# A Strassen matmul with RMS norm: GpSimd's adds to VectorE, row scaling to ScalarE, a plain last product, held row loads

## The chip, the cores and the metric

The kernel runs on one core of one Trainium2 chip. The metric is the device time of one execution in microseconds (us); lower is better. Three unprofiled runs of the kernel before took 246.84, 244.57 and 247.59 us: median 246.84.

## The reference

A product of two 2048 x 2048 matrices of float32, followed by a division of each row by its root mean square and a multiplication of each column by gamma:

```python
x = np.matmul(a, b)
rms = np.sqrt(np.mean(x ** 2, axis=-1, keepdims=True) + eps)
return (gamma * x / rms).astype(np.float32)
```

## The kernel before, in words

**Tiling.** The 2048 rows of `a` are 16 row blocks of 128; the 2048 columns of the result are four chunks of 512 (`CH`), two per half (`HALF` = 1024). A matmul instruction multiplies a 128x128 tile of `a` (transposed, it is the stationary operand) by a 128x512 tile of `b` into one PSUM bank. Depth is 16 tiles (`KT`), or 8 pairs (`KP`). `b` is kept whole in SBUF as bf16, `raw[j][kp]`, j being the half of the columns. Seven PSUM banks rotate as accumulators (`new_bank`, L304), an eighth serves transposes.

**Head (row blocks 0 to 3).** While `a` and `b` stream in by GpSimd's DMA queue (`load_head`, `load_b`, `load_later`), TensorE transposes four row blocks and multiplies them plainly (`head_matmul`, L300): first the left half of the columns, then the right half of blocks 0 to 2 (L350 to L357), then the two right chunks of block 3 (`r3`, L385 to L398). Meanwhile VectorE forms sums of quarters of `b` (`b_sums`, L218; `b_sums_in_place`, L225, which overwrites the two off-diagonal quarters of `raw[j][kp]` with sums).

**Strassen groups (row blocks 4 to 15).** Groups g = 2 (`G0`) to 7 hold two row blocks each, ra = 2g and rb = 2g+1. Each is done in two column halves, j = 0 and j = 1. A half (`group_half`, L401) is one level of Strassen's method: seven products of 8 matmuls in place of eight, in the order 2, 5, 1, 4, 3, 7, 6 (`product`, L230). Products 4 and 3 go on accumulating in the banks of products 2 and 5 (`start=False`), so product 4 can't start until ScalarE has copied product 2 out of its bank into the tile `t` (L414), and product 3 not until VectorE has added product 5 to `t` (L417). The four result chunks x11, x12, x21, x22 (t is x22's tile) come from these lines:

- L414 ScalarE copies product 2 to t; L417 and L421 VectorE adds product 5 and subtracts t from product 1;
- L424 ScalarE copies product 4 to x21 and squares it; L426 **GpSimd** forms x11 = t + x21;
- L429 ScalarE copies product 3 to x12 and squares it; L431 **GpSimd** forms t = t + x12;
- L435 and L440 VectorE adds products 7 and 6 to x11 and x22; ScalarE squares both.

`square` (L255) also accumulates the sum of squares of a row into `msq`. `finish(mb)` (L296) turns the four sums of a row block into 1/rms (VectorE reduce L271, add of eps L273, ScalarE square root L278, VectorE reciprocal L281), multiplies two halves of 1024 columns by it and by gamma on VectorE (L291), and writes each out by SyncE's queue (L294).

**Row blocks of a group to come.** Rows arrive by `load_block` (L116, GpSimd's queue, two float32 buffers `a32`). `row_norm` (ScalarE, L184 and L187) takes the norm of each row, `row_scale` (VectorE, L192 to L201) turns it to a power of two and writes the scaled rows as fp16 to `a16`, and `transpose_dma` (L173, SyncE's queue) transposes them by DMA into `at(mb)`. VectorE then forms the five sums of quarters of `a` that products 1, 2, 5, 6, 7 take (`a_sums`, L207 to L213).

**Order.** The schedule is written by hand: every engine works through its instructions in program order, and `hooks_of(g, j)` (L443) names the extra work that stands after each product of a half: hook n is placed between products. For j = 0 of a group from 3 on: hook 0 row_scale and transpose of block 2g+2, hook 1 row_norm of 2g+3, hook 3 row_scale and transpose of 2g+3 and finish of 2g-2. For j = 1: hook 0 the two row loads, hook 2 finish of 2g-1, hook 3 a_sums 2, 5, 1 of the next group, hook 5 row_norm of 2g+4, hooks 6 and 7 a_sums 7 and 6.

**Last half.** `last_half` (L491 on) is group 7, j = 1: the same seven products, with gamma multiplied in early, adds and multiplications on GpSimd (L517, L518, L523, L533), and five writes at the end (L534 to L546).

Of the kernel before, what the change touches and what calls it, by code (L numbers as in the profile page):

```python
# [17 lines left out]
def kernel(  # L18
# [156 lines left out]

    norm = {}
    eps_of = {}
# [12 lines left out]
    def row_scale(mb):  # L190
# [5 lines left out]
        e = stat_pool.tile([P, 1], FP32, name="e")  # L196
        nc.vector.tensor_scalar(out=e, in0=s, scalar1=s, scalar2=float(eps),
                                op0=ALU.mult, op1=ALU.mult)
        eps_of[mb] = e
        a16[mb] = a16_slot(mb)  # L200
        nc.vector.tensor_scalar_mul(out=a16[mb], in0=a32.pop(mb), scalar1=s)  # L201
# [23 lines left out]
    def b_sums_in_place(j, kp, eng=nc.vector):  # L225

        flat = raw[j][kp].rearrange("p t n -> p (t n)").rearrange("p (q n) -> p q n", q=4)
        eng.tensor_tensor(out=flat[:, 1:3, :], in0=flat[:, 1:3, :], in1=flat[:, 0::3, :],
                          op=ALU.add)
# [15 lines left out]
    msq = {}  # L245
    n_sq = {}

    def square(mb, src):
        if mb not in msq:
            msq[mb] = stat_pool.tile([P, NCH], FP32, name="msq")  # L250
            n_sq[mb] = 0
# [16 lines left out]
    def partial_rms(mb):  # L268

        part = stat_pool.tile([P, 1], FP32, name="part")  # L270
        nc.vector.reduce_sum(out=part, in_=msq[mb][:, 0:NCH - 1], axis=mybir.AxisListType.X)  # L271
        e = eps_of.pop(mb, None)
        nc.vector.tensor_scalar_add(out=part, in0=part, scalar1=float(eps) if e is None else e)  # L273
        return part

    def inverse_rms(mb, part):
        rms = stat_pool.tile([P, 1], FP32, name="rms")
        nc.scalar.activation(out=rms, in_=msq.pop(mb)[:, NCH - 1:NCH], func=ACTF.Sqrt,  # L278
                             bias=part, scale=1.0)
# [7 lines left out]
    def finish(mb):  # L287
        r = inverse_rms(mb, partial_rms(mb))
# [59 lines left out]
    for kp in range(KP):  # L348
# [12 lines left out]
        if kp == 4:  # L361
            row_norm(HB)
            row_scale(HB)
# [3 lines left out]
        if kp == 6:  # L367
            row_norm(HB + 1)
            row_scale(HB + 1)
# [6 lines left out]
    for r in range(HB - 1):  # L376
        for c, copy in ((2, nc.scalar.copy), (3, nc.vector.tensor_copy)):
            copy(out=x_chunk(r, c), in_=banks[r, c])

# [3 lines left out]

    squares2(0)
    r3 = HB - 1  # L385
    bank = new_bank()
    for kt in range(KT):
        head_matmul(bank, r3, 2, kt)
    finish(0)
    a_sums(G0, (2, 5, 1))  # L390
    squares2(1)
    nc.scalar.copy(out=x_chunk(r3, 2), in_=bank)
    bank = new_bank()
    for kt in range(KT):
        head_matmul(bank, r3, 3, kt)
# [192 lines left out]
```

## Time and profile before

| | us |
|---|---|
| median of three runs | 246.84 |
| the profiled execution, whole | 246.81 |
| its span in the profile | 245.0 |
| PE (TensorE) busy in the span | 217.9 |
| DVE (VectorE) busy | 179.8 |
| ACT (ScalarE) busy | 109.7 |
| POOL (GpSimd) busy | 82.8 |

The profile names engines PE, DVE, ACT, POOL and SP (SyncE); SPq, ACTq and POOLq are their queues. A row of the timeline gives the start and the length of an instruction in us, the engine, the line, the operation, the tile written and the tiles read, and in brackets how long the engine had been idle before it and what ended that. A wait row gives the engine and tile that waited, what it waited for, the total, the count and the longest. A window row gives, for a stretch of the span, each engine's busy time, the granted TensorE clock (1.00 is full) and what the DMA engines moved. The times of consecutive instructions overlap somewhat: an engine starts the next one before the last has left its pipeline, so the step from start to start is shorter than the length shown.

### The profile page before, as it was taken

The page shows a single profiled execution, that of the slowest core. Times are in us where ns is not written, and L with a number is a line of the kernel's source. Part 1 is how long each engine was busy: PE and PEld are TensorE (multiplying, and loading weights), DVE is VectorE, ACT ScalarE, POOL GpSimd, SP SyncE. Part 2 cuts the span into 40 slices and gives each one's busy share as a digit, 9 for nine tenths or more (in the row PEclk, how much of TensorE's full clock was granted, in tenths as well). Part 3 has the DMA queues.
Part 4 walks back from the last instruction along what each step waited for, and adds up shares of the span by engine and source line. Part 5 has one row for each costly group of instructions (what it writes and reads, how often), then busy time and mean ns, then how long its engine had stood idle before and what let it go on. Part 6 is the DMA issues. An engine that isn't in the chain of part 4 may idle for free.

```text
span 245.0 us, 2997 instructions
## 1 busy us (share of the span) xinstructions
PE 217.9 (89%) x1033; PEld 99.1 (40%) x1033; DVE 179.8 (73%) x304; ACT 109.7 (45%) x256; POOL 82.8 (34%) x71
## 2 busy tenths in 40 slices
PE   6789999998994999894999999999999999999800
PEld 1345444444441344341444444444444444444300
DVE  1144459835789989999868995999599959597760
ACT  3100004685279323627536843784377434343440
POOL 8333332100039417050354144504350515050640
PEclk9999999999997699998999999999999999999985
DMA  6999999999643068834889098809881934044026
GB/s 192 200 206 204 209 206 209 298 292 262 268 183 150 0 131 244 358 126 171 155 298 400 15 184 294 372 16 200 283 361 24 184 137 171 1 173 174 1 100 243
DMA packets 36560, 47.13 MB, mean 192 GB/s; under 512 B 21952, under 2 KB 26560, under 8 KB 34880
## 3 DMA queue, kind: packets, MB, share of 16 engines
q0 software_dynamic: 9648, 23.33, 37.4%
q1 hardware_dynamic: 26320, 21.50, 28.5%
q10 hardware_dynamic: 576, 2.10, 2.5%
q8 instruction: 8, 0.13, 0.2%
q14 instruction: 8, 0.07, 0.1%
HBM read 34.60 MB, written 16.78 MB: 210 GB/s over the span
## 4 chain that ended last, share of the span: by engine, by line
PE 57%; DVE 21%; DMA 13%; issue 3%; ACT 2%; POOL 2%; DVEq 0%; ACTq 0%; POOLq 0%
PE acc L238 46%; PE acc L301 10%; DMA b_7_84<-in_b_dram 7%; DMA b_3_80<-in_b_dram 6%; DVE s_105 L213 2%; DVE s_103 L213 2%; DVE early L223 1%; DVE s_104 L213 1%; DVE x_99 L291 1%; POOL early L107 1%; PE tbank L166 1%; DVE at_even L170 1%; DVE head_at L201 1%; ACT rms L278 1%; DVE x_102 L522 1%
## 5 line engine op out<-in xcount | busy, mean ns | idle before, releaser
L301 PEld LDWEIGHTS <-head_at 128*128 128x128 bf16 x256 | 24.9, 99 | 30.6 <-issue 2.6
L278 ACT ACTIVATE rms<-msq,part 128x1 f32<-128x1 f32 x16 | 4.7, 294 | 32.7 <-DVE part L273 32.6
L238 PEld LDWEIGHTS <-head_at 128*128 128x128 f16 x96 | 9.7, 101 | 16.1 <-issue 5.7
L238 PEld LDWEIGHTS <-s_104 128*128 128x128 f16 x96 | 9.6, 101 | 16.0 <-DVE s_104 L213 3.9
L426 POOL TENSOR_TENSOR x_97<-x_101 128x512 f32<-128x512 f32 x3 | 5.7, 1908 | 30.3 <-ACT x_101 L424 30.3
L238 PE MATMUL acc<-t_left,head_at 128*128 128x512 bf16 x48 | 12.2, 412 | 3.5 <-ACT x_101 L414 3.5
L426 POOL TENSOR_TENSOR x_95<-x_99 128x512 f32<-128x512 f32 x3 | 6.3, 2098 | 26.6 <-ACT x_99 L424 26.6
L238 PEld LDWEIGHTS <-s_105 128*128 128x128 f16 x96 | 9.7, 101 | 12.4 <-issue 1.9
L337 ACT COPY x_95<-acc 128x512 f32<-128x512 f32 x2 | 1.1, 589 | 30.4 <-PE acc L301 30.4
L238 PEld LDWEIGHTS <-at_even 128*128 128x128 f16 x96 | 9.4, 98 | 12.5 <-issue 1.2
L157 DVE COPY head_at<-tbank 128x1024 bf16<-128x1024 bf16 x7 | 4.8, 692 | 12.9 <-PE tbank L152 12.9
L238 PEld LDWEIGHTS <-s_107 128*128 128x128 f16 x96 | 9.4, 98 | 11.3
L238 PEld LDWEIGHTS <-s_106 128*128 128x128 f16 x96 | 9.4, 98 | 11.3
L238 PEld LDWEIGHTS <-s_103 128*128 128x128 f16 x96 | 9.4, 98 | 11.3
L426 POOL TENSOR_TENSOR x_96<-x_100 128x512 f32<-128x512 f32 x3 | 4.8, 1588 | 21.3 <-ACT sq L255 21.3
L238 PE MATMUL acc<-early,at_even 128*128 128x512 bf16 x48 | 10.8, 379 | 1.0 <-ACT x_100 L414 1.0
L238 PE MATMUL acc<-early,s_103 128*128 128x512 bf16 x48 | 11.3, 380 | 0.0
L238 PE MATMUL acc<-t_left,s_103 128*128 128x512 bf16 x48 | 11.3, 380 | 0.0
L238 PE MATMUL acc<-t_left,at_even 128*128 128x512 bf16 x48 | 10.9, 379 | 0.0
L238 PE MATMUL acc<-early,head_at 128*128 128x512 bf16 x48 | 10.8, 380 | 0.0
L255 ACT ACTIVATE sq<-x_95 128x512 bf16<-128x512 f32 x8 | 5.0, 631 | 8.1 <-DVE x_95 L435 8.0
L255 ACT ACTIVATE sq<-x_97 128x512 bf16<-128x512 f32 x8 | 5.0, 628 | 7.5 <-DVE x_97 L435 7.4
(320 smaller groups left out, 594.5 us busy)
## 6 DMA issues: line engine op xcount, KB each, us to landing
out_dram<-x_95 SPq DMA_DIRECT2D x4, 512.0 KB, 3.0
out_dram<-x_99 SPq DMA_DIRECT2D x4, 512.0 KB, 3.8
out_dram<-x_96 SPq DMA_DIRECT2D x4, 512.0 KB, 2.7
out_dram<-x_100 SPq DMA_DIRECT2D x4, 512.0 KB, 4.0
out_dram<-x_97 SPq DMA_DIRECT2D x4, 512.0 KB, 3.2
early<-in_a_dram POOLq DMA_DIRECT2D x7, 256.0 KB, 15.8
out_dram<-x_101 SPq DMA_DIRECT2D x3, 512.0 KB, 3.5
out_dram<-x_98 SPq DMA_DIRECT2D x3, 512.0 KB, 2.7
```

What stands on the lines that cost most here:

```text
L107: nc.gpsimd.dma_start(out=ah(kp), in_=a[0:HB * P, kp * W2:(kp + 1) * W2].rearrange("(r p) k -> p r k", p=P))
L157: nc.vector.tensor_copy(out=head_at[:, 2 * kp:2 * kp + 2, :, :], in_=view)
L166: nc.tensor.matmul(view[:, n, :], a16[mb][:, kt * P:(kt + 1) * P], identity_h, is_transpose=True, start=(n == 0), stop=(n == 7),)
L170: nc.vector.tensor_copy(out=at(mb)[:, g * 8:(g + 1) * 8, :], in_=view)
L201: nc.vector.tensor_scalar_mul(out=a16[mb], in0=a32.pop(mb), scalar1=s)
L213: nc.vector.tensor_tensor(out=s_sum[s], in0=x, in1=y, op=op)
L223: nc.vector.tensor_tensor(out=sums[j][:, n, kp, :], in0=x, in1=y, op=op)
L238: nc.tensor.matmul(bank, lhsT[:, kp, :], rhs, start=(start and kp == 0), stop=(kp == KP - 1), skip_group_check=not start)
L255: nc.scalar.activation(out=sq[:, 0:CH], in_=src, func=ACTF.Square, scale=inv_sqrt_n, accum_out=msq[mb][:, c:c + 1])
L278: nc.scalar.activation(out=rms, in_=msq.pop(mb)[:, NCH - 1:NCH], func=ACTF.Sqrt, bias=part, scale=1.0)
L301: nc.tensor.matmul(bank, head_at[:, kt, r, :], head_rhs(c, kt), start=(kt == 0), stop=(kt == KT - 1))
L426: nc.gpsimd.tensor_tensor(out=x11, in0=t, in1=x21, op=ALU.add)
```

## The change

1. The two adds of a Strassen half that GpSimd did (L426, L431) are VectorE's; so are the four `b_sums_in_place` that it did.
2. `row_scale` is split into `row_factor` (VectorE, four small operations; the scaled eps goes straight into an extra column of `msq`) and `row_apply` (the scaling of 2048 columns), which is VectorE's for blocks 4 to 7 and ScalarE's from block 8 on. For groups from 3 on they stand at hooks 0, 1, 3 and 4 of j = 0.
3. `finish` sums five columns of `msq` (eps is one) and takes the root of that: one VectorE operation fewer, and the reduce now needs all four squares.
4. At the entrance to the groups, the copies of the last head banks, a_sums, finish(0), row_norm of blocks 6 and 7, and the squares stand in another order; TensorE's order is the same. In group 2, finishes and `b_sums` stand at other hooks.
5. `load_after`: before the loads of the two row blocks for the group after next, GpSimd copies one column of the tile x22 of j = 0, which holds the loads until VectorE has written that tile.
6. The last half is a plain product: four chunks of 16 matmuls. The two quarters of `b` that had been overwritten by sums are loaded again (`load_again`, at hook 3 of j = 1 of group 6) into the two row buffers. Row block 14 is finished by `finish`; block 15's chunks are kept one by one, the last one straight from its bank, and written in four pieces of 512 columns.

The diff, cut to its core:

```diff
+    msq = {}
+    n_sq = {}
+
+    def new_msq(mb):
+        msq[mb] = stat_pool.tile([P, NCH + 1], FP32, name="msq")
+        n_sq[mb] = 0
+
+    for mb in range(HB):
+        new_msq(mb)
+        nc.gpsimd.memset(msq[mb][:, NCH:], float(eps))
+
+
...
-    def row_scale(mb):
+    def row_factor(mb):
         s = stat_pool.tile([P, 1], FP32, name="s")
         nc.vector.tensor_scalar_max(out=s, in0=norm.pop(mb), scalar1=1e-18)
         nc.vector.reciprocal(out=s, in_=s)
         nc.vector.tensor_single_scalar(out=s.bitcast(I32), in_=s.bitcast(I32),
                                        scalar=0x7F800000, op=ALU.bitwise_and)
-        e = stat_pool.tile([P, 1], FP32, name="e")
-        nc.vector.tensor_scalar(out=e, in0=s, scalar1=s, scalar2=float(eps),
+        new_msq(mb)
+        nc.vector.tensor_scalar(out=msq[mb][:, NCH:], in0=s, scalar1=s, scalar2=float(eps),
                                 op0=ALU.mult, op1=ALU.mult)
-        eps_of[mb] = e
+        factor[mb] = s
+
+    def row_apply(mb):
         a16[mb] = a16_slot(mb)
-        nc.vector.tensor_scalar_mul(out=a16[mb], in0=a32.pop(mb), scalar1=s)
+        if mb < HB + 4:
+            nc.vector.tensor_scalar_mul(out=a16[mb], in0=a32.pop(mb), scalar1=factor.pop(mb))
+        else:
+            nc.scalar.activation(out=a16[mb], in_=a32.pop(mb), func=ACTF.Copy,
+                                 scale=factor.pop(mb))
...
+    def inverse_rms(mb, partial=None):
+
         rms = stat_pool.tile([P, 1], FP32, name="rms")
-        nc.scalar.activation(out=rms, in_=msq.pop(mb)[:, NCH - 1:NCH], func=ACTF.Sqrt,
-                             bias=part, scale=1.0)
+        m = msq.pop(mb)
+        if partial is None:
+            tot = stat_pool.tile([P, 1], FP32, name="tot")
+            nc.vector.reduce_sum(out=tot, in_=m, axis=mybir.AxisListType.X)
+            nc.scalar.activation(out=rms, in_=tot, func=ACTF.Sqrt)
+        else:
+            nc.scalar.activation(out=rms, in_=m[:, NCH - 1:NCH], func=ACTF.Sqrt,
+                                 bias=partial, scale=1.0)
...
-    for r in range(HB - 1):
-        for c, copy in ((2, nc.scalar.copy), (3, nc.vector.tensor_copy)):
-            copy(out=x_chunk(r, c), in_=banks[r, c])
-
     def squares2(r):
         for c in (2, 3):
             square(r, x_chunk(r, c))
 
+    x_right = [[x_chunk(r, c) for c in (2, 3)] for r in range(HB - 1)]
+    for c in range(2):
+        nc.scalar.copy(out=x_right[0][c], in_=banks[0, 2 + c])
     squares2(0)
+    a_sums(G0, (2, 5))
+    finish(0)
+    nc.scalar.copy(out=x_right[1][0], in_=banks[1, 2])
+    for r, c in ((1, 1), (2, 0), (2, 1)):
+        nc.vector.tensor_copy(out=x_right[r][c], in_=banks[r, 2 + c])
+    a_sums(G0, (1,))
+    row_norm(HB + 2)
+    squares2(1)
+
     r3 = HB - 1
-    bank = new_bank()
-    for kt in range(KT):
-        head_matmul(bank, r3, 2, kt)
-    finish(0)
-    a_sums(G0, (2, 5, 1))
-    squares2(1)
-    nc.scalar.copy(out=x_chunk(r3, 2), in_=bank)
-    bank = new_bank()
-    for kt in range(KT):
-        head_matmul(bank, r3, 3, kt)
-    row_norm(HB + 2)
+    for c in (2, 3):
+        bank = new_bank()
+        for kt in range(KT):
+            head_matmul(bank, r3, c, kt)
+        nc.scalar.copy(out=x_chunk(r3, c), in_=bank)
+        if c == 2:
+            row_norm(HB + 3)
     squares2(2)
-    nc.scalar.copy(out=x_chunk(r3, 3), in_=bank)
...
-        nc.gpsimd.tensor_tensor(out=x11, in0=t, in1=x21, op=ALU.add)
+        nc.vector.tensor_tensor(out=x11, in0=t, in1=x21, op=ALU.add)
...
-        nc.gpsimd.tensor_tensor(out=t, in0=t, in1=x12, op=ALU.add)
+        nc.vector.tensor_tensor(out=t, in0=t, in1=x12, op=ALU.add)
...
+    pace = consts.tile([P, 1], FP32, name="pace")
+
+    def load_after(g, mb):
+
+
+        nc.gpsimd.tensor_copy(out=pace, in_=x_chunk(2 * g + 1, 1)[:, 0:1])
+        load_block(mb)
...
-        def scale(mb):
-            row_scale(mb)
+        def apply(mb):
+            row_apply(mb)
             transpose_dma(mb)
 
         more = g + 1 < NG
         if j == 0:
-            if more:
-                hook(0, scale, nxt)
-                hook(0 if g == G0 else 1, row_norm, nxt + 1)
             if g == G0:
-                for kp in range(KP // 2):
-                    hook(0, b_sums_in_place, 1, kp, nc.gpsimd)
+                hook(0, row_factor, nxt)
+                hook(0, apply, nxt)
+                hook(0, row_factor, nxt + 1)
                 hook(1, squares2, r3)
-                hook(1, a_sums, g, (7, 6))
-            if more:
-                hook(3, scale, nxt + 1)
-            if g == G0:
+                hook(2, apply, nxt + 1)
+                hook(2, a_sums, g, (7, 6))
                 hook(3, b_sums_in_place, 0, KP - 1)
                 hook(3, finish, 1)
-                hook(4, b_sums, 1, KP - 1)
+                hook(4, finish, 2)
+                hook(6, b_sums, 1, KP - 1)
+            elif more:
+                hook(0, row_factor, nxt)
+                hook(1, apply, nxt)
+                hook(1, row_norm, nxt + 1)
+                hook(3, row_factor, nxt + 1)
+                hook(3, finish, 2 * g - 2)
+                hook(4, apply, nxt + 1)
             else:
                 hook(3, finish, 2 * g - 2)
-                if not more:
-                    hook(5, finish, 2 * g - 1)
+                hook(5, finish, 2 * g - 1)
         else:
             if g == G0:
-                for kp in range(KP // 2, KP):
-                    hook(1, b_sums_in_place, 1, kp)
-            if g == G0:
-                hook(2, finish, 2)
-                hook(5, finish, r3)
+                for kp in range(KP):
+                    hook(1 + kp // 4, b_sums_in_place, 1, kp)
             else:
                 hook(2, finish, 2 * g - 1)
             if more:
                 hook(3, a_sums, g + 1, (2, 5, 1))
                 hook(6, a_sums, g + 1, (7,))
                 hook(7, a_sums, g + 1, (6,))
+            if g == G0:
+                hook(4, finish, r3)
             if g + 2 < NG:
-                hook(0, load_block, nxt + 2)
+                hook(0, load_after, g, nxt + 2)
                 hook(0, load_block, nxt + 3)
                 hook(5, row_norm, nxt + 2)
+            elif more:
+                hook(3, load_again)
         return hooks
 
+
+
+    b_again = {}
+
+    def load_again():
+        nc.gpsimd.tensor_copy(out=pace, in_=x_chunk(MB - 3, 1)[:, 0:1])
+
+        for q, cols in ((2, (2 * CH, 3 * CH)), (1, (3 * CH, N))):
+            raw_q = a_pool.tile([P, K], FP32, name="a32").bitcast(BF16)
+            b_again[q] = raw_q.rearrange("p (k n) -> p k n", n=CH)
+            rows_q = b.rearrange("(k t p) n -> p t k n", t=2, p=P)[:, q // 2]
+            nc.gpsimd.dma_start(out=b_again[q], in_=rows_q[:, :, cols[0]:cols[1]])
+
     def last_half():
...
+        def chunk(mb, c):
+            bank = new_bank()
+            for kt in range(KT):
+                q = 2 * (kt % 2) + c % 2
+                rhs = b_again[q][:, kt // 2] if q in b_again else b_quarter(1, kt // 2, q // 2, q % 2)
+                nc.tensor.matmul(bank, at(mb)[:, kt], rhs, start=(kt == 0), stop=(kt == KT - 1))
+            return bank
+
+        def keep(mb, c, bank):
+            x = x_chunk(mb, c)
+            nc.scalar.copy(out=x, in_=bank)
+            square(mb, x)
+
+        keep(ra, 2, chunk(ra, 2))
+        keep(ra, 3, chunk(ra, 3))
+        x = x_tile(rb, 0)
+        nc.vector.tensor_tensor(out=x, in0=x, in1=gamma_sb[:, 0:HALF], op=ALU.mult)
+        keep(rb, 2, chunk(rb, 2))
+        nc.vector.tensor_tensor(out=x_chunk(rb, 2), in0=x_chunk(rb, 2), in1=gam[2], op=ALU.mult)
+        finish(ra)
+        part = stat_pool.tile([P, 1], FP32, name="part")
+        nc.vector.tensor_scalar(out=part, in0=msq[rb][:, 0:1], scalar1=msq[rb][:, 1:2],
+                                scalar2=msq[rb][:, 2:3], op0=ALU.add, op1=ALU.add)
+        nc.vector.tensor_tensor(out=part, in0=part, in1=msq[rb][:, NCH:], op=ALU.add)
+        bank = chunk(rb, 3)
+        square(rb, bank)
+        r = inverse_rms(rb, part)
+        y = [x_chunk(rb, c) for c in range(NCH)]
+        nc.scalar.activation(out=y[0], in_=y[0], func=ACTF.Copy, scale=r)
+        nc.scalar.dma_start(out=rows(rb, 0, CH), in_=y[0])
+        nc.vector.scalar_tensor_tensor(out=y[3], in0=bank, scalar=r, in1=gam[3],
                                       op0=ALU.mult, op1=ALU.mult)
+        nc.sync.dma_start(out=rows(rb, 3 * CH, N), in_=y[3])
+        for c, queue in ((1, nc.sync), (2, nc.scalar)):
+            nc.vector.tensor_scalar_mul(out=y[c], in0=y[c], scalar1=r)
+            queue.dma_start(out=rows(rb, c * CH, (c + 1) * CH), in_=y[c])
```

75 lines of the change are left out of this document (10 added, 65 removed).

## The prediction

> **What bounds the kernel now.** I read the stretches first, cut where TensorE's work changes:
>
> ```profile
> 0.00:36.90 36.90, 31.97 (x171) 15.48 (x172) 13.66 (x32) 2.52 (x3) 15.95 (x27) 1.00 1.10 203
> ...
> 74.30:119.55 45.25, 37.32 (x154) 15.80 (x153) 43.30 (x66) 21.62 (x53) 16.52 (x9) 0.89 0.51 164
> 119.55:219.69 100.14, 100.14 (x465) 45.33 (x464) 82.63 (x130) 56.08 (x134) 36.81 (x24) 1.00 0.61 193
> 219.69:231.95 12.26, 12.26 (x57) 5.38 (x55) 9.23 (x14) 4.53 (x11) 3.66 (x3) 1.00 0.26 105
> 231.95:245.00 13.05, 0.00 (x0) 0.00 (x0) 4.13 (x8) 3.18 (x7) 3.36 (x2) 0.69 0.43 161
> ```
>
> After span and matmuls the columns are PE, PEld, DVE, ACT, POOL, clock, DMA share, GB/s. From 119.55 to 231.95 TensorE never pauses, at full clock: whatever other engines do there is worth nothing. Two stretches can give: 74.30 to 119.55, and the 13.05 us after the last matmul. Before 74.3 TensorE's order stays and the change moves nothing that its loads or transposes wait for. TensorE's waits and its timeline say what the first loses:
>
> ```profile
> PE acc L238 <- ACT x_101 L414: 3.5, 1, 3.5
> PE acc L238 <- DVE s_104 L213: 3.4, 1, 3.4
> PE acc L238 <- ACT x_100 L414: 1.0, 1, 1.0
> ```
> ```profile
> 73.90 0.59 PE L301 MATMUL acc<-b_7_92,head_at 128*128 128x512 bf16 x2
> 77.92 0.61 PE L238 MATMUL acc<-b_0_77,s_104 128*128 128x512 bf16 x1 [3.43 <-DVE s_104 L213]
> ...
> 83.40 0.38 PE L238 MATMUL acc<-b_5_82,s_105 128*128 128x512 bf16 x1
> ...
> 98.99 3.61 PE L238 MATMUL acc<-early,at_even 128*128 128x512 bf16 x16 [0.96 <-ACT x_100 L414]
> ...
> 109.34 1.89 PE L238 MATMUL acc<-t_left,s_103 128*128 128x512 bf16 x8
> 114.77 4.94 PE L238 MATMUL acc<-t_left,head_at 128*128 128x512 bf16 x16 [3.54 <-ACT x_101 L414]
> 119.55 0.38 PE L238 MATMUL acc<-b_0_77,s_107 128*128 128x512 bf16 x1
> ```
>
> At full clock a matmul takes 12.08/56 = 0.2157 us (the last half's 56, counted 12.26 with the last one's drain of 0.17), a product of 8 takes 1.73, a half 12.08. After 3.4 and 3.5 us of idleness matmuls run at half rate for a while: 77.92 to 83.40 holds 13 in 5.48, not 2.80 (2.68 lost), 114.77 to 119.55 holds 16 in 4.78, not 3.45 (1.33 lost). After 0.96 there is no loss. From start to start each wait is 0.16 longer than its idle time (109.34 + 1.73 = 111.07, to 114.77 is 3.70; likewise 3.59 and 1.12). Together 3.59 + 2.68 + 1.12 + 3.70 + 1.33 = **12.4 us** could go.
>
> **Why they stand there.** The first wait is for a sum on VectorE that takes 2.61 where the same sum takes 0.68 elsewhere, while GpSimd adds beside it (the multiply at 145.13, 2.30 for 1.28, is another case):
>
> ```profile
> 71.34 2.91 POOL L228 TENSOR_TENSOR b_0_85<-b_0_85 128x1024 bf16<-128x1024 bf16 x1 [5.11 <-PE acc L301]
> ```
> ```profile
> 75.26 2.61 DVE L213 TENSOR_TENSOR s_104<-at_even 128x1024 f16<-128x1024 f16 x1
> ...
> 130.81 0.68 DVE L421 TENSOR_TENSOR x_102<-acc,x_102 128x512 f32<-128x512 f32 x1
> 131.41 0.68 DVE L213 TENSOR_TENSOR s_104<-at_even 128x1024 f16<-128x1024 f16 x1
> ...
> 137.45 0.14 DVE L192 TENSOR_SCALAR s<-norm 128x1 f32<-128x1 f32 x1
> ...
> 138.14 1.28 DVE L201 TENSOR_SCALAR head_at<-a_1074,s 128x2048 f16<-128x2048 f32 x1
> ...
> 142.97 0.15 DVE L271 TENSOR_REDUCE part<-msq 128x1 f32<-128x3 f32 x1
> ...
> 143.73 0.16 DVE L281 RECIPROCAL r<-rms 128x1 f32<-128x1 f32 x1 [0.36 <-ACT rms L278]
> 143.93 1.28 DVE L291 SCALAR_TENSOR_TENSOR x_97<-x_97,r,gamma_sb 128x1024 f32<-128x1024 f32 x1
> 145.13 2.30 DVE L291 SCALAR_TENSOR_TENSOR x_98<-x_98,r,gamma_sb 128x1024 f32<-128x1024 f32 x1
> ```
>
> The other two are copies of t (L414) late on ScalarE, behind squares that wait for VectorE.
>
> **Prices**, as steps from start to start. VectorE: a sum or add 0.60 (130.81 to 131.41), a finish multiply 1.20 (143.93 to 145.13), a scaling as long as that (1.28), 1.20, factor 0.70 (137.45 to 138.14). The two adds taken from GpSimd read SBUF twice and have no free row on VectorE: as the PSUM add, 0.60, to half a finish multiply, 0.60; both ends agree. A finish: reduce 0.22, root 0.33 (143.40 to 143.73), reciprocal 0.20, two multiplies: 3.15. ScalarE:
>
> ```profile
> 137.02 0.63 ACT L255 ACTIVATE sq<-x_102 128x512 bf16<-128x512 f32 x1 [0.54 <-DVE x_102 L440]
> ...
> 137.65 0.57 ACT L414 COPY x_99<-acc 128x512 f32<-128x512 f32 x1
> 138.11 1.06 ACT L184 ACTIVATE sq<-a_1076 128x1024 bf16<-128x1024 f32 x1
> ...
> 140.47 0.29 ACT L187 ACTIVATE norm<-n_1198 128x1 f32<-128x1 f32 x1
> ...
> 143.40 0.29 ACT L278 ACTIVATE rms<-msq,part 128x1 f32<-128x1 f32 x1 [2.63 <-DVE part L273]
> ```
> ```profile
> L540 ACT ACTIVATE x_101<-x_101,r 128x1024 f32<-128x1024 f32 x1 | 1.1, 1148 | 0.3 <-DVE r L281 0.3
> ```
>
> A copy takes 0.48, 0.62 until its reader starts; a square 0.63, or 0.75 ahead of another (half of the norm's 2.36, less 0.43 for the 512 columns more); a norm 2.57 with its root. Scaling 2048 columns on ScalarE has no row. Squares grow by 0.43 per 512 columns (0.63, 1.06); two such steps more on the 1148 ns row give 2.0, a step of 1.92. Bounds: 1.8 (the square's 1.06 and two steps, less 0.1 of overlap) and 2.5 (four squares of 512). I take 1.92, from the row that scales.
>
> **The order laid out by hand**, each engine in program order with those prices, a product's reader starting 0.25 after TensorE can go on (200.70 + 1.73 = 202.43 to 202.68):
>
> ```profile
> 200.70 3.62 PE L238 MATMUL acc<-early,at_even 128*128 128x512 bf16 x16
> ...
> 202.68 0.58 ACT L424 COPY x_100<-acc 128x512 f32<-128x512 f32 x1 [2.12 <-PE acc L238]
> ```
>
> GpSimd no longer adds, so a sum costs 0.60 and the first group's s_2 is ready at 69: TensorE goes from 74.3 straight on. What decides next is again the copy of t, due 0.1 before product 4:
>
> | half | what stands ahead | t copied | TensorE due | wait |
> |---|---|---|---|---|
> | group 2, left | ScalarE from 66.1: 5 copies 2.4, 6 squares 4.5, norms 6 and 7 5.1, root 0.2, 1.3 of waiting for finish 0's reduce: 79.6 | 80.2 | 79.5 | 0.7 |
> | group 2, right | VectorE from 80.2: finish 1 and 2 6.3, 9 adds and sums 5.4, `b_sums(1, 7)` 1.1, a scaling 1.2: 94.2; then a square and the copy | 95.7 | 93.3 | 1.0 + 2.5 |
> | group 3, left | VectorE from 94.2: 8 in-place sums 4.8, 10 adds and sums 6.0, finish 3 3.15: 108.15; then a square and the copy | 109.7 | 107.8 | 1.9 |
> | group 3, right | ScalarE from 109.5: scaling, norm, VectorE's factor and reduce, root, copy, square, scaling, copy: 119.2; two adds 1.4, two squares 1.5, the copy | 122.65 | 121.8 | 0.9 |
> | group 4, left | VectorE from 122.65: finish 5, 10 adds and sums: 131.8; then a square and the copy | 133.3 | 134.7 | 0 |
> | group 4, right | as in group 3 | 146.3 | 146.8 | 0 |
>
> The 1.0 is product 1 of group 2, right: its last two matmuls need `b_sums(1, 7)`, now behind finish 2. New waits 0.7 + 1.0 + 2.5 + 1.9 + 0.9 = 7.0, so 12.4 - 7.0 = **5.5 us** won (unrounded), and the last half starts at 214.2, not 219.69. From group 4 a round from t to t takes 12.97 us for a left half and 10.68 for a right one, 23.65 against TensorE's 24.16: hidden with 0.5 us of cover. VectorE's two adds (1.2 a half), ScalarE's scalings (3.8 a group) and the finishes ride in that round and cost nothing while it is the shorter; beyond it each us costs one per group.
>
> **What else costs nothing.** The eps column's four memsets on GpSimd come while its queue waits for loads. On SyncE's queue the second transpose of a group moves behind the two writes of finish(2g-2); their last multiply ends at 141.6 in group 4, before the scaled rows (142.2).
>
> **Held loads.** The small copy on GpSimd waits for x22 of the left half, 144.6 in group 4, 15.1 after the group's start. Only the two load issues queue behind it on GpSimd. Rows of before (the last line is over all writes of the result):
>
> ```profile
> a_1293<-in_a_dram POOLq DMA_DIRECT2D x1, 1024.0 KB, 6.5
> a_1295<-in_a_dram POOLq DMA_DIRECT2D x1, 1024.0 KB, 8.5
> out_dram<-x_101 ACTq DMA_DIRECT2D x1, 512.0 KB, 3.8
> out_dram<-x_98 ACTq DMA_DIRECT2D x1, 512.0 KB, 5.6
> head_at<-head_at SPq DMA_TRANSPOSE x6, 4.4
> ```
> ```profile
> DMA to landing us min/median/max: 2.6/3.1/6.5
> ```
>
> They land at 151.2 and 153.2; the norm wants the first at 151.9. The second transpose, 142.2 + 4.4 = 146.6, is 4 us ahead of the sums at 150.7. Nothing on the path, though the loads start 2 us before that transpose is through. The reloaded quarters (2.1 MB written) are asked for about 192 and wanted at 214.4 and 217.6: with 2.1 MB of output among them, 4.2 MB at the 203 GB/s of the first 36.9 us, in which loads were never short of requests, take 20.7 us: to 213. They just fit.
>
> **The end.** GpSimd's adds and multiplies there go (L517 to L533), and eight matmuls come: 8 x 0.2157 = **+1.7**. TensorE ends at 228.1. Then, in the chain as before, square and root: block 15's third chunk is copied by 225.3, its gamma multiply (0.6), finish(14) (3.15) and the partial sum (0.4) hold VectorE to 229.4, later than the last square (228.9); root to 229.8, reciprocal 230.0, three multiplies of 0.6, 0.4 and 0.4 (512 columns; a third of a scaling's 1.20) to 231.5; the last write of 256 KB goes out at 231.6. Now:
>
> ```profile
> 237.54 0.36 ACTq L546 DMA_DIRECT2D out_dram<-x_98  x1
> ```
>
> It landed 5.6 later, at 243.1, and the span ran on 1.9 to 245.0. With half as much written behind the last matmul I take 3.8 (the x_101 row, 512 KB with others queued; bounds 2.6, the shortest write, and 5.6): 235.4, plus 1.9 is 237.2. The tail is 9.1, not 13.05: **-3.95**.
>
> Sum: 245.0 - 5.5 + 1.7 - 3.95 = 237.2; with 1.8 around the span (246.81 - 245.0) **239.0 us**. The profiled 246.81 and the median 246.84 are the same, so this is 3.2% under the median.
>
> **A rule weighed.** The 2.5 us wait lies between the rows with loss (3.4) and without (0.96). The Trainium skill, "TensorE: Matmul & The Clock Gate", Part 1, says that the clock falls to half after about one idle window of 3.4 us; the two rows agree. By that rule the wait costs no clock and the sum stays 239.0; by the row of 77.92 it would be 241.7.
>
> **Rivals.**
> A. *ScalarE and VectorE become the bound.* The round has 0.5 us of cover. With a scaling of 2.5 it is 24.8: 0.65 too long in groups 4 to 6, and 1.15 more in group 3; TensorE ends 3.1 later: **242.1 us**. For: the cover is thin, and 0.02 us more on each step of the two engines use it up as well. Against: the 1148 ns row. 20%.
> B. *A cold clock at the entrance.* The 2.5 us wait follows a 1.0 wait closely; if it halves the clock as after 3.43, 2.7 us are lost: **241.7 us**. 12%.
> C. *Slower: held loads come too late.* The norm would block ScalarE, with squares and the next t behind it. First load lands 6.5 after issue; the norm has 0.7, t then 1.9, of cover. From 2.6 us late on, each us costs one in each of four groups. At 13 us: (6.5 - 2.6) x 4 = 15.6, **254.6 us**; slower by 2% needs 12 us. Against: the loads of the rows above took 6.5 and 8.5. 4%.
> D. *The reload is late.* At 165 GB/s the second quarter lands at 217.5 and from there on each us late is one lost; at 145 GB/s it is 221; TensorE waits 3 us: **242 us**. 6%.
>
> **How the numbers follow.** My forecast (5.5 and 4 us won, 1.7 paid) has 58%, and its own scatter is +-2. The range reaches down to a scaling of 1.8, shorter waits and a tail with 2.6 (236.5, with the runs' scatter of 1.5 down to 235.0), up to A with a little more: 244.0. A measurement tells about 2% of this kernel from no change, 241.9 downwards. Faster: 0.53 of the forecast's 0.58, half of B and D, 0.09, and 0.12 of A's milder forms: 0.74. Slower: C and a hundredth for worse forms of A: 0.05. Same: 0.21.
>
> **What would show it.** Right: no GpSimd add; VectorE sums at 0.68 throughout; the wait for s_104 gone; waits for L414's copy of 0.5 to 2.5 us in groups 2 and 3 and none from group 4 on; the last half starting near 214, 64 matmuls, a tail near 9. Wrong: TensorE waiting once per group after 130 (A), matmuls 0.43 apart near 96 (B), norms waiting for loads (C), a wait for the reloaded quarters (D), or a tail that is still 12 us.

## The result and the profile after

The changed kernel takes 236.98 us (median of four runs, 236.82 to 237.10) against 246.54 us (four runs, 244.57 to 247.59): a ratio of 0.962, 95% interval 0.956 to 0.968. It is faster, by 3.8%; 239.0 us had been predicted. Times here are medians over the executions of a kernel; where some took over 1.5% longer than the quickest, as in run 5, the time and the ratio are those of the quicker ones.

The stretches of the changed kernel, cut at the same events as those of before (columns as there):

```profile
36.90:74.06 37.16, 35.83 (x188) 17.08 (x189) 26.76 (x59) 21.97 (x51) 3.57 (x6) 1.00 0.95 266
74.06:112.00 37.94, 35.06 (x151) 15.36 (x153) 32.43 (x61) 22.20 (x51) 3.38 (x3) 0.96 0.53 177
112.00:212.40 100.40, 99.59 (x454) 45.29 (x463) 74.10 (x137) 69.18 (x144) 5.69 (x12) 1.00 0.83 219
212.40:226.40 14.00, 13.93 (x64) 6.17 (x63) 5.66 (x9) 5.58 (x14) 0.00 (x0) 1.00 0.19 77
226.40:235.30 8.90, 0.00 (x0) 0.00 (x0) 3.69 (x8) 1.70 (x4) 0.00 (x0) 0.63 0.61 236
```

The last half starts at 212.40, 7.3 us before 219.69. It is 14.00 long for 12.26, and the tail 8.90 for 13.05. So -7.3 + 1.7 - 4.15 = -9.7, the whole difference of the two spans (235.3 and 245.0). DMA share in the third stretch rises from 0.61 (in 119.55 to 219.69) to 0.83, the bytes only from 193 to 219 GB/s. The reload is new there; why the DMA engines are busy so much longer no run shows.

TensorE's timeline, where it waits:

```profile
77.51 1.89 PE L256 MATMUL acc<-t_left,s_103 128*128 128x512 bf16 x8
79.47 3.61 PE L256 MATMUL acc<-t_left,at_even 128*128 128x512 bf16 x16
...
89.83 1.67 PE L256 MATMUL acc<-early,s_103 128*128 128x512 bf16 x7
91.97 0.38 PE L256 MATMUL acc<-early,s_103 128*128 128x512 bf16 x1 [0.46 <-DVE early L241]
94.53 5.30 PE L256 MATMUL acc<-early,at_even 128*128 128x512 bf16 x16 [2.18 <-ACT x_100 L431]
99.66 0.38 PE L256 MATMUL acc<-b_0_85,s_107 128*128 128x512 bf16 x1
...
120.89 3.40 PE L256 MATMUL acc<-early,head_at 128*128 128x512 bf16 x14 [0.28 <-ACT x_102 L431]
```

The wait of 3.4 us for s_104 is gone, and so is the one of 3.5 us for the copy of x_101. What is left are four of the five waits that the prediction laid out, smaller; after 121 TensorE waits for nothing. Behind the 2.18 us of idleness 16 matmuls take 99.66 - 94.53 = 5.13, not 3.45: 1.68 lost, at a granted clock of 0.67 in that stretch.

Rows of ScalarE, VectorE and GpSimd: the scaling (L218), an add that was GpSimd's (L448), and the held loads (L466 is the small copy, L116 a load).

```profile
108.21 2.00 ACT L218 ACTIVATE head_at<-a_848,s 128x2048 f16<-128x2048 f32 x1
110.12 1.04 ACT L196 ACTIVATE sq<-a_850 128x1024 bf16<-128x1024 f32 x1
```
```profile
90.29 0.68 DVE L448 TENSOR_TENSOR x_99<-x_99,x_95 128x512 f32<-128x512 f32 x1
90.90 0.68 DVE L452 TENSOR_TENSOR x_95<-acc,x_95 128x512 f32<-128x512 f32 x1
```
```profile
93.25 2.38 POOL L466 COPY pace<-x_99 128x1 f32<-128x1 f32 x1 [27.28 <-DVE x_99 L457]
95.57 0.53 POOL L116 DMA_DIRECT2D a_848<-in_a_dram  x1
...
119.53 0.18 POOL L466 COPY pace<-x_101 128x1 f32<-128x1 f32 x1 [22.90 <-DVE x_101 L457]
120.06 0.53 POOL L116 DMA_DIRECT2D a_1072<-in_a_dram  x1 [0.34 <-issue]
```

From start to start the scaling takes 1.91 and an add 0.61. Next come some DMA issues (the last figure is the time from issue to landing in us), the landing times of the transposes (L173), and the end:

```profile
a_1763<-in_b_dram POOLq DMA_DIRECT2D x1, 1024.0 KB, 12.5
a_1765<-in_b_dram POOLq DMA_DIRECT2D x1, 1024.0 KB, 19.5
out_dram<-x_102 ACTq DMA_DIRECT2D x1, 256.0 KB, 3.7
```
```profile
DMA to landing us min/median/max: 4.2/4.7/7.0
```
```profile
226.47 0.60 ACT L268 ACTIVATE sq<-acc 128x512 bf16<-128x512 f32 x1 [1.14 <-PE acc L547]
...
228.52 0.29 ACT L290 ACTIVATE rms<-msq,part 128x1 f32<-128x1 f32 x1 [1.35 <-DVE part L565]
...
230.62 0.35 ACTq L577 DMA_DIRECT2D out_dram<-x_102  x1
```

### The profile page after: what moved, and what is told of

Same layout as the page of the kernel before. It is cut to its first block, busy times and chain, and to the rows that moved or that the text cites. A ratio compares the mean times of both kernels' runs of the same rounds, so it can differ in the third digit from the quotient of the medians.

```text
span 235.3 us, 2970 instructions
## 1 busy us (share of the span) xinstructions
PE 215.1 (91%) x1021; PEld 99.0 (42%) x1041; DVE 156.6 (67%) x303; ACT 123.2 (52%) x264; POOL 28.7 (12%) x52
## 5 line engine op out<-in xcount | busy, mean ns | idle before, releaser
L256 PE MATMUL acc<-early,at_even 128*128 128x512 bf16 x47 | 12.5, 422 | 2.2 <-ACT x_100 L431 2.2
L288 ACT ACTIVATE rms<-tot 128x1 f32<-128x1 f32 x15 | 3.0, 203 | 21.5 <-DVE tot L287 21.5
L256 PEld LDWEIGHTS <-s_107 128*128 128x128 f16 x88 | 8.6, 98 | 10.4
L256 PEld LDWEIGHTS <-s_106 128*128 128x128 f16 x88 | 8.6, 98 | 10.4
L256 PEld LDWEIGHTS <-s_103 128*128 128x128 f16 x88 | 8.6, 98 | 10.4
L256 PEld LDWEIGHTS <-s_104 128*128 128x128 f16 x88 | 8.6, 98 | 10.4
L256 PEld LDWEIGHTS <-s_105 128*128 128x128 f16 x88 | 8.6, 98 | 10.4
L256 PEld LDWEIGHTS <-head_at 128*128 128x128 f16 x80 | 7.8, 98 | 10.0 <-issue 0.8
L256 PE MATMUL acc<-t_left,head_at 128*128 128x512 bf16 x48 | 10.8, 379 | 0.0
L256 PE MATMUL acc<-early,s_103 128*128 128x512 bf16 x40 | 9.6, 379 | 0.5 <-DVE early L241 0.5
L547 PEld LDWEIGHTS <-head_at 128*128 128x128 f16 x64 | 6.3, 98 | 7.5
L466 POOL COPY pace<-x_99 128x1 f32<-128x1 f32 x2 | 2.6, 1284 | 49.3 <-DVE x_99 L457 49.3
L204 DVE TENSOR_SCALAR s<-norm 128x1 f32<-128x1 f32 x12 | 1.8, 150 | 9.0 <-ACT norm L199 9.0
L256 PE MATMUL acc<-early,head_at 128*128 128x512 bf16 x31 | 7.2, 379 | 0.3 <-ACT x_102 L431 0.3
```

The source lines that it names most:

```text
L204: nc.vector.tensor_scalar_max(out=s, in0=norm.pop(mb), scalar1=1e-18)
L256: nc.tensor.matmul(bank, lhsT[:, kp, :], rhs, start=(start and kp == 0), stop=(kp == KP - 1), skip_group_check=not start)
L288: nc.scalar.activation(out=rms, in_=tot, func=ACTF.Sqrt)
L466: nc.gpsimd.tensor_copy(out=pace, in_=x_chunk(2 * g + 1, 1)[:, 0:1])
L547: nc.tensor.matmul(bank, at(mb)[:, kt], rhs, start=(kt == 0), stop=(kt == KT - 1))
```

## The experiments

Theory at the start: the gain at the entrance comes from GpSimd's adds and sums going and from the new order, the end brings some 2 us, and the held loads cost and bring nothing. Rivals: the hold is what pays, or the scaling on ScalarE. "After" is the changed kernel, "before" the other one; ratios are to runs of before on the same chip. "The hold" is the small GpSimd copy ahead of the row loads, "the entrance" the stretch from the end of the head to group 3.

### 1. The two adds back on GpSimd

```diff
-        nc.vector.tensor_tensor(out=x11, in0=t, in1=x21, op=ALU.add)
+        nc.gpsimd.tensor_tensor(out=x11, in0=t, in1=x21, op=ALU.add)
...
-        nc.vector.tensor_tensor(out=t, in0=t, in1=x12, op=ALU.add)
+        nc.gpsimd.tensor_tensor(out=t, in0=t, in1=x12, op=ALU.add)
```

> The changed kernel, with only the two adds of each Strassen half back on GpSimd. My theory: the 9.6 us come from two places, 7.3 up to the start of the last half (VectorE no longer slowed by GpSimd, and its work at the entrance of groups 2 and 3 in another order) and 2.5 at the end (shorter tail, less the 8 matmuls). By it the adds on GpSimd stretch VectorE's sums and finish multiplies again (0.68 to 1.7, 1.28 to 2.3), VectorE is the engine that is never idle in group 2, so the waits there grow by 1.5 to 3 us, and the round of ScalarE and VectorE, which had 0.5 us of cover, overruns in groups 3 to 6: 239 to 243 us. Rival (the adds only moved, TensorE hides them as it did before): 237 +-0.5.

239.13 us (ratio 0.968, 0.965 to 0.972), 2.15 over after and at the lower end of what I expected. Beside a GpSimd add a pair of finish multiplies takes 3.49 us, where run 7 has 2.48. The wait for b_sums grows from 0.46 to 1.28, and groups 4 and 5 get waits of 0.58 and 0.17 for sums. The waits of before do not come back: with the hold in place the adds alone are worth some 2 us.

### 2. The old last half

`last_half` as before, without `load_again`; the rest is after's.

> The changed kernel with the last half of the kernel before (seven products, GpSimd's adds and multiplications, five writes) and no second load of b. My theory: TensorE ends 1.7 us earlier, the tail is 13.05 again instead of 8.9: 237.0 - 1.7 + 4.15 = 239.4 us. Rival (the end gives nothing, everything came from the entrance): 235.3 us or 237.

239.96 us (ratio 0.972, 0.969 to 0.976): the plain end is worth 3.0 us here, in keeping with 4.15 - 1.74 = 2.4 from the two traces.

### 3. No hold

```diff
-        nc.gpsimd.tensor_copy(out=pace, in_=x_chunk(2 * g + 1, 1)[:, 0:1])
         load_block(mb)
```

> The changed kernel without the small GpSimd copy ahead of the row loads, so that they start as soon as their buffers are free. My theory: neither loads nor transposes are on TensorE's path (4 us of cover for the second transpose, 1.2 for the load): 237.0 +-0.5, the trace showing loads some 8 us earlier and transposes longer than the 4.7 us of now. Rival (the hold is what the change needs): transposes slowed past their 4 us of cover, sums late, 0.5 to 2 us per group lost, 239 to 245.

255.75 us (ratio 1.037, 1.031 to 1.043): 18.8 us over after, and slower than before. My theory fell, and the rival's 239 to 245 was too low as well. Rows of SyncE's queue, of ScalarE, the landing times of the transposes, and rows of TensorE:

```profile
81.16 10.96 SPq L173 DMA_TRANSPOSE head_at<-head_at  x1
92.21 5.29 SPq L306 DMA_DIRECT2D out_dram<-x  x4
```
```profile
103.21 0.59 ACT L431 COPY x<-acc 128x512 f32<-128x512 f32 x1 [9.46 <-DMA out_dram<-x]
```
```profile
DMA to landing us min/median/max: 4.2/11.5/19.5
```
```profile
103.85 5.22 PE L256 MATMUL acc<-early,at_even 128*128 128x512 bf16 x16 [11.76 <-ACT x L431]
138.91 3.63 PE L256 MATMUL acc<-b,s 128*128 128x512 bf16 x16 [2.21 <-DVE s L231]
...
166.27 3.63 PE L256 MATMUL acc<-b,s 128*128 128x512 bf16 x16 [2.03 <-DVE s L231]
```

The loads now go out at 76.97 and 81.63 (after: 95.57 and 96.09), beside the transposes. A transpose takes 11.5 us to land (median) instead of 4.7, and its issue holds SyncE's queue for up to 10.96. Four output writes stand behind it. The copy of t needs the tile that one of them reads: it waits 9.46 for that write, and TensorE 11.76 for the copy. At groups 4 to 6 TensorE waits 1.7 to 2.2 us for sums of late transposes.

### 4. All scaling on VectorE

```diff
-        if mb < HB + 4:
+        if mb < MB:
```

> The changed kernel with all row scaling on VectorE. My theory: a round of the two engines is then 22.9 us instead of 23.65, both under TensorE's 24.16 a group: 237.0 +-0.5, the scaling's place is worth nothing. Rival (VectorE, which took over GpSimd's adds, can't carry the scaling as well): waits for the copy of t or for sums from group 4 on, 0.5 to 1.5 us per group, 239 to 243.

236.39 us (ratio 0.957, 0.954 to 0.959): where the rows from block 8 on are scaled makes no difference that counts; if any, VectorE is 0.6 better. That rival fell.

### 5. Before, with nothing but the adds and sums moved to VectorE

```diff
-        nc.gpsimd.tensor_tensor(out=x11, in0=t, in1=x21, op=ALU.add)
+        nc.vector.tensor_tensor(out=x11, in0=t, in1=x21, op=ALU.add)
...
-        nc.gpsimd.tensor_tensor(out=t, in0=t, in1=x12, op=ALU.add)
+        nc.vector.tensor_tensor(out=t, in0=t, in1=x12, op=ALU.add)
...
-                    hook(0, b_sums_in_place, 1, kp, nc.gpsimd)
+                    hook(0, b_sums_in_place, 1, kp)
```

> The kernel before with one part alone: the two adds of each half and the four in-place sums of b taken from GpSimd to VectorE, nothing else. My theory: the wait for s_104 (3.6 us with 2.7 of slow clock) goes, since a sum takes 0.68 again; but VectorE's list at the entrance gets 2.4 us of sums and 1.2 us of adds per half longer in its old order, so the waits for the copy of t stay: 240 to 243 us, some 4 to 6 us won. Rival (the order is what matters, contention nothing): 246 +-1.

267.8 us (266.82 and 268.75; all four executions 266.82 to 281.13, median 273.52; ratio 1.087, 1.079 to 1.095): 21 us slower than before, where 4 to 6 us of gain had been expected. The trace is of the longest execution (span 279.4), so its waits sum to more than that. The part that was expected did come: the three sums of a whose first had made TensorE wait take 1.89 us together, where each took 2.6 in before.

```profile
73.02 1.89 DVE L213 TENSOR_TENSOR s<-at_even 128x1024 f16<-128x1024 f16 x3
```

In before, GpSimd's in-place sums stood beside them (71.34 to 82.37); its first add of a group came only at 91.03. So it was the in-place sums that made this wait. What went wrong stands in GpSimd's queue, in before and then in this run:

```profile
91.03 2.10 POOL L426 TENSOR_TENSOR x_95<-x_99 128x512 f32<-128x512 f32 x1 [8.67 <-ACT x_99 L424]
93.21 2.13 POOL L431 TENSOR_TENSOR x_99<-x_99,x_95 128x512 f32<-128x512 f32 x1
95.29 0.57 POOL L116 DMA_DIRECT2D a_840<-in_a_dram  x1
```
```profile
77.35 0.53 POOL L116 DMA_DIRECT2D a<-in_a_dram  x1 [11.46 <-DVE head_at L201]
```

In before a load stood behind the half's two adds in GpSimd's order, and so went out only at 95.29, when the transposes were through. Without the adds it goes out at 77.35, as soon as its buffer is free. Landing times of the transposes and rows of TensorE in this run:

```profile
DMA to landing us min/median/max: 4.5/12.6/24.9
```
```profile
109.94 6.49 PE L238 MATMUL acc<-early,at_even 128*128 128x512 bf16 x16 [17.99 <-ACT x L414]
147.81 6.34 PE L238 MATMUL acc<-b,s 128*128 128x512 bf16 x16 [3.75 <-DVE s L213]
184.17 5.24 PE L238 MATMUL acc<-b,s 128*128 128x512 bf16 x16 [9.30 <-DVE s L213]
```

New theory: GpSimd's adds were an unseen brake on the loads, and the hold puts it back. Runs 7 and 8 test that.

### 6. Before, with the plain end alone

This is before with `last_half` and `load_again` of after; the reload comes without its small copy.

> The kernel before with one part alone: the plain last half with the second load of two quarters of b (not held). My theory: 8 more matmuls, +1.7, and a tail of 8.9 for 13.05: 246.5 - 2.4 = 244.1 us. Rival (the reload comes late beside GpSimd's adds, or the tail was short only because GpSimd had stopped): 246 to 249.

244.51 us (10 executions; ratio 0.992, 0.989 to 0.994): the end alone brings 2.1 us, a small gain but clear of the noise. Together with run 2: 2 to 3 us.

### 7. Run 5 and the hold

```diff
+    def load_after(g, mb):
+        nc.gpsimd.tensor_copy(out=pace, in_=x_chunk(2 * g + 1, 1)[:, 0:1])
+        load_block(mb)
...
-                hook(0, load_block, nxt + 2)
+                hook(0, load_after, g, nxt + 2)
```

> The kernel before with its adds and its in-place sums on VectorE, as in the run that took 273.5 us, and in addition the small GpSimd copy ahead of the row loads. Theory (the adds on GpSimd were the brake on the loads, and nothing else in the 273.5 us comes from VectorE's extra work): the loads are issued after the last sum of the left half again, the transposes L173 land in about 5 us, the waits of 18 and 4 to 9 us go, and what is left is the gain of the adds, so 240 to 243 us, at most 244. Rival (VectorE with scaling, adds and sums is itself too full in the kernel before): 250 us or more, with waits for sums in every group although the transposes land in 5 us.

238.88 us (ratio 0.967, 0.963 to 0.972), some 29 us under run 5 for a copy of 128 numbers per group. All of TensorE's waits from 72 us on, and the landing times of the transposes:

```profile
79.53 3.61 PE L238 MATMUL acc<-t_left,at_even 128*128 128x512 bf16 x16 [0.39 <-ACT x L414]
92.32 3.61 PE L238 MATMUL acc<-early,at_even 128*128 128x512 bf16 x16 [0.55 <-ACT x L414]
107.36 4.96 PE L238 MATMUL acc<-t_left,head_at 128*128 128x512 bf16 x16 [2.80 <-ACT x L414]
```
```profile
DMA to landing us min/median/max: 4.2/4.3/4.9
```

The waits went as expected, and the time lies below my range of 240 to 243: the gain is larger than I had thought. All of this is with before's order at the entrance, its scaling and its end. The last half starts at 212.30 here (16 matmuls, 3.45 us, behind a row at 208.85) and at 212.40 in after. Run 2, which has the new order and scaling with the same end, took 239.96; the intervals of the two ratios overlap. So the adds and in-place sums on VectorE, with the hold, carry the whole gain of the entrance, and the new order with the scaling on ScalarE adds none that can be measured.

Adds and in-place sums moved together here, and no run moves the in-place sums alone. Run 1 prices the adds at 2.15 us, so most of the rest of the 7.3 us is probably theirs: the wait for s_104, which they made, cost 3.59 + 2.68 us in before.

### 8. A shorter hold

```diff
-        nc.gpsimd.tensor_copy(out=pace, in_=x_chunk(2 * g + 1, 1)[:, 0:1])
+        nc.gpsimd.tensor_copy(out=pace, in_=x_chunk(2 * g + 1, 0)[:, 0:1])
```

> The changed kernel with a shorter hold: the small copy reads the chunk that ScalarE writes after the fourth product, not the one that VectorE writes after the seventh, so the loads are issued some 10 us earlier, beside the second block's transposes but after the first's. Theory (a late transpose costs only what it is late beyond its slack; the second block's transposes have some 15 us until the sums of the next group read them): transposes beside loads take about 10 us instead of 4.7, half of them, and the time stays at 237 us, 236.5 to 237.8. Rival (any load beside a transpose blocks SP's queue and with it the output writes, as with no hold): over 241 us, with waits of ScalarE for output writes.

247.42 us (10 executions; ratio 1.002, 0.9995 to 1.004): the whole gain is gone, and my expectation that the slack covers it is wrong. Landing times of the writes (L306) between 80 and 95 us in this run, then of all transposes, then rows of TensorE:

```profile
DMA to landing us min/median/max: 4.2/9.0/10.3
```
```profile
DMA to landing us min/median/max: 4.2/4.3/11.7
```
```profile
98.01 6.32 PE L256 MATMUL acc<-early,at_even 128*128 128x512 bf16 x16 [5.50 <-ACT x L431]
...
158.82 3.63 PE L256 MATMUL acc<-b,s 128*128 128x512 bf16 x16 [1.49 <-DVE s L231]
```

In group 2 both transposes were through; here the loads, issued at 85.71, run beside four output writes, which take 9.0 us where after's four in that stretch take 2.7. ScalarE's copy of t waits 3.21 for a write, TensorE 5.50 for the copy, and 16 matmuls then take 2.7 us longer. In later groups the second transpose is up to 11.7 us on its way, and sums come late (waits of 1.49 and 1.58). So in group 2 the loads need a place after the writes as well as after the transposes, and the point that the change chose has both. In group 3 of after it has neither in full: the loads go out at 120.06, 3 us after the second transpose (7.0 to landing) and ahead of two writes (123.48 and 124.67), and TensorE waits for none of them.

### 9. Idle squares on ScalarE

This is after, with 1, 3, 4 and 2 extra squares ahead of the copy of t in the right halves of groups 3 to 6, to make idle times of chosen length on TensorE. It adds work and is slower for that reason.

> The changed kernel with 1, 3, 4 and 2 idle squares of 1024 columns (0.96 us each) put ahead of ScalarE's copy of t in the right halves of groups 3, 4, 5 and 6: TensorE waits of about 1.2, 2.4, 3.3 and 1.4 us, each alone in a dense stretch. It measures which idle time halves the clock. By the rule of one idle window of 3.4 us none does, or only the 3.3 one; by the changed kernel's own row (2.18 us idle, 0.46 shortly before, 1.7 us lost after) the 2.4 and the 3.3 do, the 1.2 and the 1.4 don't. Time 237 + 8 to 9 us of waits + 0 to 5 of slow clock.

245.18 us (one execution).

```profile
94.06 5.30 PE L256 MATMUL acc<-early,at_even 128*128 128x512 bf16 x16 [2.18 <-ACT x L435]
...
121.51 3.61 PE L256 MATMUL acc<-early,head_at 128*128 128x512 bf16 x15 [1.37 <-ACT x L435]
148.00 3.61 PE L256 MATMUL acc<-early,at_even 128*128 128x512 bf16 x15 [2.15 <-ACT x L435]
175.58 5.30 PE L256 MATMUL acc<-early,head_at 128*128 128x512 bf16 x16 [3.25 <-ACT x L435]
```

The first row is the wait that after has too. No time is lost after 1.37 and 2.15 (3.61 is the undisturbed length of 16 matmuls; a row can count 15 where a record is missing), and 1.7 us are lost after 2.18 and after 3.25. A step between 2.15 and 2.18 would fit these four rows, but not run 10 (lost after 2.07) and run 3 (nothing lost after 2.21). The two squares in group 6 were absorbed.

### 10 to 12. Another order at the entrance

Run 10 scales block 7 on ScalarE, moves the squares of block 2 behind the copy of t, and puts b_sums ahead of finish(2) and block 15's partial sum ahead of finish(14).

> A version that may beat both: the changed kernel with ScalarE scaling block 7 too, the squares of block 2 behind the copy of t, the last sums of b ahead of finish 2, and the partial sum of block 15 ahead of finish 14. My theory: VectorE's list at the entrance of group 2 is what TensorE still waits for (0.5 + 2.2 us and 1.7 us of slow clock after it). 1.2 us come off that list and it starts 1.5 us earlier, so the 2.2 us wait falls under 0.3 and the slow clock goes; a wait of up to 1.5 us comes back in group 3. The tail loses 0.4. 233.5 to 235.0 us. Rival (the list only shifts, the wait comes back in full in group 3): 236 to 237.

236.26 us (ratio 0.959, 0.954 to 0.963). The wait only shrank to 2.07:

```profile
93.61 5.30 PE L256 MATMUL acc<-early,at_even 128*128 128x512 bf16 x16 [2.07 <-ACT x L430]
```

The gain that I expected did not come. ScalarE's squares and scaling made the root of finish(1) late, and VectorE stood still for it for 1.71 us. Run 11 takes more off VectorE at the entrance. Only blocks 7 to 9 are scaled on ScalarE in it; those from 10 on go back to VectorE, as in run 4 (the diff is cut to its core):

```diff
-        if mb < HB + 4:
+        if mb not in (HB + 3, HB + 4, HB + 5):
...
+                hook(1, apply, nxt + 1)
...
+                hook(4, b_sums, 1, KP - 1)
+                hook(4, squares2, 2)
+                hook(5, squares2, r3)
+                hook(6, finish, 2, (0,))
...
+                if g == G0 + 1:
+                    hook(2, finish, r3)
...
+                hook(2, finish, 2, (1,))
```

> The changed kernel with another order at the entrance of group 2: block 7 scaled on ScalarE directly behind the first copy of t, late sums of b ahead of the finish of block 2, that finish cut in two (its first multiply in the left half, its second in the right), the finish of block 3 in the left half of group 3, the last squares behind the copies, and the partial sum ahead of the finish of block 14. Theory (the 0.46 and 2.18 us that TensorE waits near 92 and 94 us, and the 1.68 us of half clock behind them, come from VectorE's queue of finishes and sums alone): these go, less some 0.5 us of new waits, 232.5 to 234.5 us. Rival (the work only moves: VectorE is full until 109 us whatever its order): 236 to 237 us, with waits of the same sum at another place.

237.65 us (235.91 to 238.42; ratio 0.962, 0.957 to 0.967): no gain. All waits in group 2 are gone, and one stands in group 3. A row of TensorE, then one of VectorE:

```profile
119.34 5.30 PE L256 MATMUL acc<-early,head_at 128*128 128x512 bf16 x16 [3.57 <-ACT x L434]
```
```profile
108.05 0.16 DVE L293 RECIPROCAL r<-rms 128x1 f32<-128x1 f32 x1 [3.79 <-ACT rms L288]
```

VectorE was not full: it stood 3.79 us behind a root that ScalarE gave only after a scaling and a norm. Run 12 works that root out in group 2:

```diff
+    def stats(mb):
+        r_of[mb] = inverse_rms(mb)
...
+                if g == G0:
+                    hook(6, stats, r3)
```

> The order of the run before this one, with one thing moved: the statistic of block 3 (sum, root, reciprocal) is worked out in the right half of group 2, where ScalarE is idle, so that only its two multiplies stand in the left half of group 3. Theory (the run before lost its gain in one new wait: VectorE stood 3.79 us behind a root that ScalarE's scaling and norm held up, and TensorE then waited 3.57 us and ran 1.68 us longer at half clock): the root is there, the last sum of that half comes some 3.4 us earlier, the wait shrinks to about 0.2 us and the slow clock behind it goes, so 232 to 233.5 us, and the last half starts near 207.5. Rival (VectorE is full whatever the order): 235.5 to 237.5 us, with a wait of 2 us or more at another place between 77 and 125 us.

233.27 us (ratio 0.946, 0.940 to 0.953), inside the expected range, 4.4 us under run 11 for the earlier place of three small operations, and 3.7 us faster than the change. TensorE waits 0.47 and 0.29, and its last half starts at 208.10, 4.3 us earlier; the tail is 9.4 for 8.9, so the partial sum's new place brought nothing that the end shows:

```profile
104.06 3.61 PE L256 MATMUL acc<-t_left,head_at 128*128 128x512 bf16 x16 [0.47 <-ACT x L437]
```

## Why the prediction was right, and where it was not

| term | predicted | measured |
|---|---|---|
| start of the last half | 214.2 (5.5 won) | 212.40 (7.3 won) |
| eight matmuls more | +1.7 | 14.00 - 12.26 = +1.74 |
| tail | 9.1 | 8.90 |
| around the span | 1.8 | 237.04 - 235.3 = 1.74 |
| time | 239.0 | 237.04 profiled, 236.98 median |

- **Entrance: mechanism right, size off.** The term that was mis-sized is "0.7 + 1.0 + 2.5 + 1.9 + 0.9 = 7.0". From start to start it came out as 0.23, 0.63, 2.34 with 1.68 of slow clock, nothing, and 0.44: 5.3. All but the fourth wait (group 3, left) are where they were laid out. The copies of t were ready earlier (TensorE goes on at 79.47 and 94.53, where 80.2 and 95.7 had been laid out), and in group 3 TensorE, 1.68 later by the slow clock, came no sooner than the copy. So the slow clock cost nothing in the end. The prediction had left it out of its sum and came near without having seen why: that part is luck. With the 0.3 by which the head ended earlier (74.06 for 74.3) the smaller sum makes up the 1.8 won beyond the 5.5, to 0.2.
- **The end: right in sum, in part by luck.** The write took 3.7 where 3.8 had been taken. The last issue came 4.2 after TensorE's end (230.62) where 3.5 had been laid out, and the span ran on only 1.0 after that write landed where 1.9 had been taken; these two misses cancel.
- **Scaling on ScalarE: priced right** (1.91 for 1.92), so rival A fell: TensorE does not wait from group 4 on. The prediction let the scalings "ride in that round and cost nothing"; run 4 shows that their place brings nothing either.
- **Held loads: the step that failed in its reading.** "Nothing on the path" is true of what the hold costs, but the step priced the small copy and not what it stands in for. The change takes away the adds behind which the loads had waited. Without the hold that costs 18.8 us (run 3), or 21 us in before (run 5). The 5.5 us had rested on a transpose of 4.4, which only the hold preserves. Loads that come too early were no rival; loads that come too late were (C, 4%).
- **The reload fitted**: the second quarter landed 19.5 us after its issue at 191.4, near 211 (213 had been estimated), and its first matmul starts at 215.9. TensorE waits for neither quarter, so D fell.
- **Rival B came true in part.** The clock fell after the 2.18 us wait, which cost 1.68 and not 2.7, and group 3 gave that time back, so the rival's 241.7 did not follow. The rule from the Trainium skill ("TensorE: Matmul & The Clock Gate", Part 1), by which that wait costs no clock, does not hold here for the length of one idle time. The same page says that the window runs freely, and so the phase may decide; no run here shows the window itself.

The net: -7.8 from adds, in-place sums and hold (246.7 to 238.88, run 7) and -2 to -3 from the end make 10 to 11 us, a little more than the 9.6 between the medians.

## What to carry to other kernels

Before taking work off an engine, look at what stands behind it in that engine's order: a DMA issue there may be timed by nothing else, and when it starts sooner it can slow others that are on the path. Price a wait that a change adds both ways: what it costs, and what would happen without it. Once an engine has few long waits left, move single small results (a root, a reduce) that stand behind long instructions before moving the long ones.

## What the hardware showed that was not expected

- **Transposes and row loads slow each other.** Where loads are held back, a DMA transpose of 128 rows lands in 4.3 to 4.7 us (medians; before 4.4, run 7 4.3, after 4.7). Where loads of 1 MB run beside it, it takes 11.5 and 12.6 us (runs 3 and 5), and its issue holds SyncE's queue for up to 10.96 us (run 3). The twelve row loads take 15.1 us in run 5 and 7.9 in run 7 (medians). Output writes beside loads took 9.0 us for 2.7 (run 8). What the transfers contend for is left open: no run separates engines, memory and queues.
- **The clock after short idle times.** It fell after idle times of 2.07 (run 10), 2.18 (after, run 9) and 2.80 us (run 7, granted clock 0.50 from 107.36 to 110.00), and did not after 2.15 (run 9), 2.03 and 2.21 (run 3). Between 2.0 and 2.2 us the length alone does not decide. What does is open.
- **A GpSimd copy of 128 numbers** took 2.38 us at 93.25 in after, while VectorE ran its in-place sums, and 0.18 at 119.53, while VectorE was idle. The other way round, a sum on VectorE took 2.6 us beside GpSimd's in-place sums (before) and 0.68 without.
